# Closing a head's maxima as a task of its own, and two spacings of the maxima in place of one

## The chip, the cores and the metric

The kernel runs on one core of one Trainium2 chip. The metric is the device time of one execution in microseconds (us). The median of three runs of the kernel before is 1185.25 us, the lowest 1184.59 and the highest 1190.17.

## The reference, cut to what matters

Two layers of a streaming block. Each layer projects a normalised input into three token mixers (a retention, a latent attention with 8 heads called MLA, and a gated linear attention called GLA), gates their outputs with silu of further projections, and multiplies the result by an output matrix. The change touches only the MLA part, and there the maxima of its softmax:

```python
def block(args):
    qn, qp, i0 = args
    sc = (jnp.einsum('bqhd,bkhd->bhqk', qn, k_nope)
          + jnp.einsum('bqhd,bkd->bhqk', qp, k_pe)).astype(jnp.float32) * scale
    q_chunk = (i0 + jnp.arange(Q_BLOCK)) // CHUNK
    mask = key_chunk[None, :] <= q_chunk[:, None]
    sc = jnp.where(mask, sc, -jnp.inf)
    p = jax.nn.softmax(sc, axis=-1).astype(v.dtype)
    return jnp.einsum('bhqk,bkhe->bqhe', p, v)
```

The sequence has 1024 positions, the model 1024 columns. Everything is float32; a full product is made of three matmuls (high by high, high by low, low by high parts).

## The kernel before, in words

TensorE's work is issued in the order in which the program is written (`manual_schedule` for PE in `body`); the order of the instructions on VectorE, ScalarE, GpSimd and the DMA queue of SyncE is made by a planner, which works on a modelled time.

In `layer`, a layer runs through the retention's projections and core, the MLA's keys and queries, then a row of projections in which the rest is woven: `gk` (GLA keys), `gv` (GLA values, `proj_v`), the gates `gz0`, `gz1` of the GLA and `mz0` to `mz3` of the MLA. After these come the MLA's values `mla_v` ("mv" in the rows), its heads (`mla`, "mhead"), and the output matrix (`out_half`, "wo").

**Ticks and tasks.** After each group of three matmuls of a projection (`proj`), or of six in `proj_v`, `tick` (L527) is called. It takes 1 off the waiting count of every task in `self.tasks`, and as long as a task's count is zero or less, lets it run to its next `yield`, whose value is added to the count. A task is so woven between the matmuls of the projections. `drain` (L543) runs a task to its end on the spot, with nothing between its steps. From `gk` to the end of `mz3` there are 16 + 32 + 6 times 16 = 144 ticks.

**The maxima.** The softmax subtracts a row maximum that is found ahead of the heads by `mla_max` (L1194), started as the task `big` with a waiting count of 8 ahead of `gk`. For each of the 8 heads it makes 12 products: query block i (128 rows) against the keys up to its end, in pieces of at most 512 columns (L1245, 6 of 512 columns and 2 each of 384, 256 and 128). Each product goes into a PSUM buffer of one of two pools in turn (`maxp`, two buffers a pool, so four), and VectorE reduces it to one column (L1247). Between two products stands `yield MAXW`, 1.15 ticks. Two pairs of SBUF tiles hold the high parts of a head's queries and keys; `load(h + 1)` stands at the head's start.

**Closing a head** (`close`, L1210): VectorE reduces the head's 16 columns to 8 (L1213), 7 ticks later TensorE turns them into rows (L1217), ScalarE negates them (L1219), and a DMA writes them to `mxd` (L1220), from where `mla_stack` fetches them as a row of the head's stacked queries (L1170). Before, this runs inside `mla_max` by `yield from` ahead of the next head's third product (i == 2), so no product is made in those 7 ticks, nor in the 1.15 ticks that follow.

**Around it.** While the maxima run, the task `prep` (`gla_prep`, under `gv`) does the GLA's decay factors on VectorE, ScalarE and GpSimd ("glap"), then the task `core` (`gla_core`, under `gz0` and `gz1`, "glac") does the gated attention, then `head_out` ("hout") puts its output in place under `mz1`. In layer 0 alone, `next_chunk("k")` ahead of `mz0` adds eight reductions of `ada_w` on VectorE ("ada"). Under `mz3` the task `first` makes the first four score tiles of the MLA heads. Then `layer` fetches the stacks of heads 1 and 2 and calls `self.drain(big)`: whatever products are left are made there, one behind the other. `mla` follows: it drains `mla_v` of the first four heads, then fills seven score tiles ahead.

Of the kernel before, what the change touches and what calls it, by code (L numbers as in the profile page):

```python
# [33 lines left out]
FOLLOW = (4, 5, 6, 7)  # L34
LAG = 7
SHIFT_PE = 5
MAXW = 1.15
RW = (18, 6)

RQ, RK, RV, RZ = 0, 256, 512, 768  # L40
# [122 lines left out]
class Builder:  # L163
# [1031 lines left out]
    def mla_max(self, l):  # L1195

        nc = self.nc
        self.lab = "mmax_"
        sets = [{n: self.sl(dt=F32R, name="mx" + n) for n in "qk"} for _ in range(2)]
        for st in sets:  # L1200
            for i, n in enumerate("kq"):
                nc.sync.dma_start(st[n][96:104, :].bitcast(F32), self.mrows[i, 1:9])
            nc.sync.dma_start(st["k"][64:96, :].bitcast(F32), self.kr[l][0])

        def load(h):
            self.lab = "mmax_"
            for n in "qk":
                self.head_rows(l, h, n, 0, sets[h % 2][n])

        def close(h, mx):  # L1210
            self.lab = "mmax_"
            m8 = self.sm([128, 8])
            nc.vector.tensor_reduce(m8, mx, AX.X, ALU.max)  # L1213
            yield 7
            self.lab = "mmax_"
            ps = self.ps()
            nc.tensor.matmul(ps[0:8, 0:128], m8, self.cst("ident"), start=True, stop=True)  # L1217
            mr = self.smp.tile([8, 128], F32R, tag="mr", name=self.nm("mr"), bufs=2)
            nc.scalar.activation(mr, ps[0:8, 0:128], AF.Copy, scale=-1.0)  # L1219
            nc.sync.dma_start(self.mxd[l][h].rearrange("o (a b) -> (o a) b", a=8), mr.bitcast(F32))  # L1220

        load(0)
        done = None
        for h in range(MH):
            yield MAXW
            st = sets[h % 2]
            if h + 1 < MH:
                load(h + 1)
            self.lab = "mmax_"
            mx = self.smp.tile([128, 8, 2], F32, tag="mx", name=self.nm("mx"), bufs=2)  # L1230
            nc.gpsimd.memset(mx, NEG)
            for i in range(8):
                n = 128 * (i + 1)
                for j in range((n + 511) // 512):
                    if i or j:
                        yield MAXW
                    if i == 2 and done:
                        yield from close(*done)
                        done = None
                        yield MAXW  # L1240
                    self.lab = "mmax_"
                    w = min(512, n - 512 * j)
                    ps = self.ps(self.maxp[self.nmx % len(self.maxp)])
                    self.nmx += 1
                    nc.tensor.matmul(ps[:, :w], st["q"][0:104, 128 * i:128 * i + 128],  # L1245
                                     st["k"][0:104, 512 * j:512 * j + w], start=True, stop=True)
                    nc.vector.tensor_reduce(mx[:, i, j:j + 1], ps[:, :w], AX.X, ALU.max)  # L1247
            done = (h, mx)
        self.task(close(*done), 8)

    def mla_scores(self, h, hf, j):
# [217 lines left out]
    def layer(self, l, src):  # L1469
        nc = self.nc  # L1470
        self.chunks.extend([(l, 4), (l, 5)] + ([(l + 1, i) for i in (0, 2, 1, 3)] if l + 1 < DEPTH else []))
        mixed = [None] * 8
        self.maxp = ("mm", "s")
        if l > 0:
            self.banks = ("pj", "s", "acc")
            self.rx = self.ret_first(l, self.after_out)
# [45 lines left out]
        for i in range(2):  # L1522
            mixed[6 + i] = self.proj_silu(l, f"gz{i}")
            self.next_chunk("jk"[i])
        mz = [self.proj_silu(l, "mz0")]
        self.drain(core)
        self.maxp = ("mm", "s")
# [61 lines left out]
```

## Time and profile before

| what | value |
|---|---|
| median of three runs | 1185.25 us |
| the profiled execution, its time | 1184.63 us |
| its span, first to last instruction | 1182.8 us |
| TensorE busy | 1128.0 us, 95% of the span |
| VectorE busy | 796.7 us, 67% |
| ScalarE busy | 596.6 us, 50% |
| GpSimd busy | 529.5 us, 45% |
| mean granted TensorE clock | 0.977 of full speed |

Rows of the trace are in us from the span's start. A row of the timeline has start, duration, engine, line, operation, output and inputs, and in brackets the idle time of the engine ahead of it and what ended it. PE is TensorE, DVE VectorE, ACT ScalarE, POOL GpSimd, SPq the DMA queue of SyncE. A matmul's duration overlaps its neighbours; its price in a stream is the distance from start to start.

### The profile page before, as it was taken

How to read it: one execution, taken by the hardware profiler on the slowest of the kernel's cores; microseconds unless marked ns; L12 is line 12 of the kernel's file. 1: busy time of each engine (PE TensorE's matmuls, PEld its weight loads, DVE VectorE, ACT ScalarE, POOL GpSimd, SP SyncE). 2: the span in 40 equal slices, each digit the busy share in tenths (PEclk: the TensorE clock that was granted, in tenths of full speed). 3: DMA queues.
4: the chain of work that ended last, by engine and by line, in shares of the span. 5: the costliest groups of instructions: out<-in, count | busy, mean ns of one | idle time of the engine just before them, and what ended most of it. 6: DMA issues, size and time to landing. Idle time of an engine off the chain costs nothing.

```text
span 1182.8 us, 16979 instructions
## 1 busy us (share of the span) xinstructions
PE 1128.0 (95%) x5968; PEld 942.6 (80%) x5968; DVE 796.7 (67%) x1366; ACT 596.6 (50%) x1164; POOL 529.5 (45%) x459
## 2 busy tenths in 40 slices
PE   6999999998999899999999999999899999999996
PEld 4878977787878688887887898778788868888896
DVE  7866595686675656768875476666675666686754
ACT  6434334433545578853543434434256447886431
POOL 0064153643443346673555333444553334668620
PEclk8899999998999899999999999999999989999998
DMA  9816563651136434248453356355111653424722
GB/s 370 296 48 194 170 225 133 187 170 41 42 120 201 119 90 108 64 152 302 169 183 99 99 172 238 99 184 157 41 41 41 195 134 90 108 63 163 249 88 72
DMA packets 65585, 169.01 MB, mean 143 GB/s; under 512 B 10262, under 2 KB 13334, under 8 KB 65500
## 3 DMA queue, kind: packets, MB, share of 16 engines
q1 hardware_dynamic: 65500, 167.93, 44.7%
q8 instruction: 47, 0.77, 0.3%
q14 instruction: 38, 0.31, 0.1%
HBM read 125.36 MB, written 38.41 MB: 138 GB/s over the span
## 4 chain that ended last, share of the span: by engine, by line
PE 75%; DVE 12%; ACT 4%; DMA 4%; issue 3%; POOL 1%; SPq 0%; DVEq 0%; ACTq 0%; POOLq 0%
PE mhead_psacc L1296 3%; PE mhead_psacc L1294 3%; PE mhead_psacc L1295 3%; PE wo_pspj L558 2%; PE wo_pspj L556 2%; PE wo_pspj L557 2%; PE pmz_pspj L556 2%; PE wo_pss L557 2%; PE wo_pss L556 2%; PE wo_pss L558 2%; PE pmz_pspj L557 2%; PE pmz_pspj L558 2%; DVE mmax_mx L1247 2%; PE mhead_pss L1263 2%; PE mhead_pss L1262 2%
## 5 line engine op out<-in xcount | busy, mean ns | idle before, releaser
L457 POOL TENSOR_TENSOR wwo_wl<-wwo_wst,wwo_wh 128x1024 fp32r<-128x1024 f32 x27 | 69.0, 2559 | 40.6 <-ACT wwo_wh L456 40.5
L1271 POOL TENSOR_TENSOR mhead_wh<-mhead_p,mhead_wh 128x384 fp32r<-128x384 f32 (+1 forms) x48 | 58.1, 1211 | 56.7 <-DVE mhead_wh L1270 56.7
L1247 DVE TENSOR_REDUCE mmax_mx<-mmax_psmm 128x1 f32<-128x512 f32 (+1 forms) x96 | 57.3, 596 | 26.4 <-PE mmax_psmm L1245 25.6
L576 DVE SCALAR_TENSOR_TENSOR ada_aw<-ada_aw,silrow 128x512 f32<-128x512 f32 x64 | 62.0, 986 | 18.5 <-DMA ada_aw<-awc 18.2
L1276 DVE TENSOR_TENSOR mhead_ph<-mhead_pss,mhead_ph 128x512 fp32r<-128x512 f32 x48 | 33.1, 689 | 38.6 <-ACT mhead_pss L1275 38.6
L556 PE MATMUL pmz_pspj<-mkh_h,wmz_wh 128*128 128x512 f32 x128 | 52.5, 410 | 0.0
L1271 POOL TENSOR_TENSOR mhead_wl<-mhead_p,mhead_wl 128x128 fp32r<-128x128 f32 (+1 forms) x48 | 35.8, 746 | 34.1 <-DVE mhead_wl L1270 34.1
L557 PE MATMUL pmz_pspj<-mkh_h,wmz_wh 128*128 128x512 f32 x128 | 50.3, 393 | 0.0
L558 PE MATMUL pmz_pspj<-mkh_h,wmz_wl 128*128 128x512 f32 x128 | 50.1, 392 | 0.0
L558 PE MATMUL wo_pspj<-gran_mx,wwo_wl 128*128 128x512 f32 (+1 forms) x120 | 44.8, 374 | 1.7 <-POOL wwo_wl L457 1.7
L556 PE MATMUL wo_pspj<-gran_mx,wwo_wh 128*128 128x512 f32 (+1 forms) x120 | 45.3, 377 | 0.2 <-ACT wwo_wh L456 0.2
L1245 PE MATMUL mmax_psmm<-mmax_mxk,mmax_mxq 104*128 104x512 f32 (+1 forms) x96 | 38.9, 408 | 6.6 <-DVE mmax_mx L1247 5.9
L557 PE MATMUL wo_pspj<-gran_mx,wwo_wh 128*128 128x512 f32 (+1 forms) x120 | 44.8, 373 | 0.0
L556 PE MATMUL wo_pss<-gran_mx,wwo_wh 128*128 128x512 f32 (+1 forms) x120 | 44.6, 371 | 0.0
L558 PE MATMUL wo_pss<-gran_mx,wwo_wl 128*128 128x512 f32 (+1 forms) x120 | 44.1, 368 | 0.0
L557 PE MATMUL wo_pss<-gran_mx,wwo_wh 128*128 128x512 f32 (+1 forms) x120 | 44.1, 368 | 0.0
L600 ACT ACTIVATE ssq_sq<-ssq_x 128x512 f32<-128x512 f32 (+1 forms) x31 | 16.5, 534 | 51.7 <-DVE ssq_x L1373 51.7
L457 POOL TENSOR_TENSOR wrk_wl<-wrk_wst,wrk_wh 128x1024 fp32r<-128x1024 f32 x3 | 8.1, 2688 | 76.0 <-ACT wrk_wh L456 76.0
L1247 DVE TENSOR_REDUCE mmax_mx<-mmax_pss 128x1 f32<-128x256 f32 (+2 forms) x72 | 36.5, 507 | 7.5 <-PE mmax_pss L1245 6.8
L605 DVE TENSOR_TENSOR ssq_sq<-ssq_sq,ssq_sq 128x512 f32<-128x512 f32 (+1 forms) x30 | 30.5, 1017 | 14.0 <-ACT ssq_sq L600 14.0
L556 PE MATMUL pv_pspj<-wgv_wh,mkh_h 128*128 128x256 f32 x128 | 38.5, 301 | 0.0
L1274 ACT ACTIVATE mhead_ph<-mhead_pss 128x512 fp32r<-128x512 f32 x48 | 28.6, 596 | 17.6 <-PE mhead_pss L1264 17.0
(565 smaller groups left out, 4140.6 us busy)
## 6 DMA issues: line engine op xcount, KB each, us to landing
ada_aw<-awc SPq DMA_DIRECT2D x64, 256.0 KB
wwo_wst<-wo SPq DMA_DIRECT2D x32, 512.0 KB
aw<-awc SPq DMA_DIRECT2D x11, 512.0 KB
x<-xT SPq DMA_DIRECT2D x8, 512.0 KB
kn<-mk_ph SPq DMA_DIRECT2D x16, 256.0 KB
kn<-mk_pl SPq DMA_DIRECT2D x16, 256.0 KB
qn<-mq_ph SPq DMA_DIRECT2D x16, 256.0 KB
qn<-mq_pl SPq DMA_DIRECT2D x16, 256.0 KB
```

The lines of the kernel that those rows point to most:

```text
L457: (eng or nc.gpsimd).tensor_tensor(lo, src, hi.bitcast(F32), ALU.subtract)
L556: mm(ps, lh, rh, start=start, stop=False)
L557: mm(ps, lh, rl, start=False, stop=False)
L558: self.last = mm(ps, ll, rh, start=False, stop=stop)
L576: step = nc.vector.scalar_tensor_tensor(v, v, 1.0, self.silrow[:, cs], ALU.mult, ALU.mult, accum_out=t[:, 2 * j + i:2 * j + i + 1])
L1245: nc.tensor.matmul(ps[:, :w], st["q"][0:104, 128 * i:128 * i + 128], st["k"][0:104, 512 * j:512 * j + w], start=True, stop=True)
L1247: nc.vector.tensor_reduce(mx[:, i, j:j + 1], ps[:, :w], AX.X, ALU.max)
L1271: nc.gpsimd.tensor_tensor(pl, p, ph.bitcast(F32), ALU.subtract)
L1276: nc.vector.tensor_tensor(pl, s, ph.bitcast(F32), ALU.subtract)
L1294: mm(acc[:, o], vh, ph, start=(j == 0), stop=False, skip_group_check=True)
L1295: mm(acc[0:64, o], vl, ph, start=False, stop=False, skip_group_check=True)
L1296: mm(acc[:, o], vh, pl, start=False, stop=last, skip_group_check=True)
```

## The change

Three things are changed, for both layers:

- `close` becomes a task of its own, added ahead of the next head's second product (i == 1), so that products go on beside it. Its TensorE step stands 6 ticks behind its reduction (7 before). The extra `yield` behind it goes.
- The spacing is `self.maxw`: 1.45 ticks from the start of the layer, and 0.95 from the end of `gz1` on (1.15 throughout before).
- Nothing else: the products, reductions, pools of PSUM, and the place of `drain(big)` are the same.

```diff
-MAXW = 1.15
+MAXW = (1.45, 0.95)
@@ close, in mla_max
             nc.vector.tensor_reduce(m8, mx, AX.X, ALU.max)
-            yield 7
+            yield 6
@@ the loop over heads, blocks and pieces, in mla_max
-            yield MAXW
+            yield self.maxw
...
                     if i or j:
-                        yield MAXW
-                    if i == 2 and done:
-                        yield from close(*done)
+                        yield self.maxw
+                    if i == 1 and done:
+                        self.task(close(*done))
                         done = None
-                        yield MAXW
@@ layer
-        self.maxp = ("mm", "s")
+        self.maxp, self.maxw = ("mm", "s"), MAXW[0]
...
         for i in range(2):
             mixed[6 + i] = self.proj_silu(l, f"gz{i}")
             self.next_chunk("jk"[i])
+        self.maxw = MAXW[1]
         mz = [self.proj_silu(l, "mz0")]
```

Stepping the tick rule by hand gives the number of products (L1245) that are made in each stretch of a layer:

| stretch | ticks | products before | products after |
|---|---|---|---|
| gk | 16 | 6 | 5 |
| gv | 32 | 20 | 22 |
| gz0 | 16 | 8 | 11 |
| gz1 | 16 | 7 | 11 |
| mz0 | 16 | 9 | 17 |
| mz1 | 16 | 12 | 17 |
| mz2 | 16 | 6 | 13 |
| mz3 | 16 | 7 | 0 |
| drain behind mz3 | 0 | 21 | 0 |

## Rows read from the trace of the kernel before

**Rows 1.** The page, part 1: engine, busy us, share of the span, instructions.
```profile
PE 1128.0 (95%) x5968; PEld 942.6 (80%) x5968; DVE 796.7 (67%) x1366; ACT 596.6 (50%) x1164; POOL 529.5 (45%) x459
```

**Rows 2.** Timeline of TensorE, layer 0, from the last of mz3 to the heads.
```profile
391.38 0.34 PE L1245 MATMUL mmax_psmm<-mmax_mxk,mmax_mxq 104*128 104x384 f32 x1
...
398.16 0.60 PE L1217 MATMUL mmax_psmm<-cst,mmax_sm 128*8 128x128 f32 x2 [2.02 <-DVE mmax_sm L1213]
...
403.03 0.41 PE L556 MATMUL mv_pspj<-wukvv_wh,pmz_lat 128*128 128x256 f32 x1
...
407.44 0.40 PE L1262 MATMUL mhead_pss<-pmz_stkqh,pmz_stkkh 105*128 105x512 f32 x1
```

**Rows 3.** Timeline of VectorE in the same stretch: reductions one behind the other.
```profile
392.24 0.68 DVE L1247 TENSOR_REDUCE mmax_mx<-mmax_pss 128x1 f32<-128x512 f32 x1
392.83 0.68 DVE L1247 TENSOR_REDUCE mmax_mx<-mmax_psmm 128x1 f32<-128x512 f32 x1
```

**Rows 4.** Timeline of TensorE, layer 1, the same place.
```profile
955.49 0.34 PE L1245 MATMUL mmax_psmm<-mmax_mxk,mmax_mxq 104*128 104x384 f32 x1
...
967.14 0.42 PE L556 MATMUL mv_pspj<-wukvv_wh,pmz_lat 128*128 128x256 f32 x1
...
972.00 0.28 PE L558 MATMUL mv_pspj<-wukvv_wh,pmz_lat 128*128 128x256 f32 x1
972.12 0.40 PE L1262 MATMUL mhead_pss<-pmz_stkqh,pmz_stkkh 105*128 105x512 f32 x1
```

**Rows 5.** Stages of 2 us: PE, PEld, DVE, ACT, POOL busy, PEclk, DMA share, GB/s.
```profile
276.00:278.00 2.00, 2.00 (x10) 2.00 (x11) 1.84 (x5) 0.00 (x0) 0.07 (x1) 0.50 0.31 109
...
312.00:314.00 2.00, 2.00 (x8) 1.52 (x7) 0.08 (x1) 0.97 (x2) 0.52 (x1) 0.54 0.60 129
...
394.00:396.00 2.00, 1.63 (x6) 0.74 (x4) 2.00 (x5) 0.16 (x1) 0.00 (x0) 1.00 0.73 166
...
398.00:400.00 2.00, 1.84 (x5) 1.25 (x6) 0.69 (x4) 0.27 (x1) 0.35 (x2) 0.50 0.91 223
```

**Rows 6.** Timeline of TensorE in mz2 of layer 1: only the maxima shown.
```profile
937.38 0.39 PE L1245 MATMUL mmax_psmm<-mmax_mxk,mmax_mxq 104*128 104x512 f32 x1
938.31 0.22 PE L1245 MATMUL mmax_pss<-mmax_mxk,mmax_mxq 104*128 104x128 f32 x1
939.11 0.40 PE L1245 MATMUL mmax_psmm<-mmax_mxk,mmax_mxq 104*128 104x512 f32 x1
```

**Rows 7.** Stages of layer 0 (columns as in Rows 5): gv with prep, then mz0 and mz1.
```profile
251.00:276.00 25.00, 21.60 (x161) 19.65 (x159) 23.27 (x41) 9.31 (x21) 12.04 (x14) 0.97 0.26 75
335.00:365.00 30.00, 28.34 (x135) 22.60 (x134) 26.24 (x53) 13.78 (x27) 11.48 (x9) 1.00 0.59 189
```

**Rows 8.** The same stages, the maxima's tile alone: DVE busy, POOL busy, PEclk, DMA.
```profile
251.00:276.00 25.00, 5.86 (x13) 0.12 (x1) 0.97 0.26 75
335.00:365.00 30.00, 10.92 (x23) 0.23 (x2) 1.00 0.59 189
```

**Rows 9.** Timeline of TensorE, layer 0: its waits under gv, gz0 and mz0.
```profile
272.33 0.50 PE L1245 MATMUL mmax_pss<-mmax_mxk,mmax_mxq 104*128 104x512 f32 x1 [1.07 <-DVE mmax_mx L1247]
275.87 0.48 PE L1245 MATMUL mmax_psmm<-mmax_mxk,mmax_mxq 104*128 104x128 f32 x1 [2.33 <-DVE mmax_mx L1247]
...
311.03 1.10 PE L1009 MATMUL glac_psacc<-pv_v,pgz_gat 128*128 128x64 f32 x8 [1.68 <-DVE mmax_mx L1247]
...
341.95 0.33 PE L1245 MATMUL mmax_psmm<-mmax_mxk,mmax_mxq 104*128 104x128 f32 x1 [0.37 <-DVE mmax_mx L1247]
```

**Rows 10.** Timeline of ScalarE behind mz3 in layer 0: the silu of mz3's second half.
```profile
392.20 0.63 ACT L430 ACTIVATE pmz_zt<-pmz_mz 128x512 f32<-128x512 f32 x1
...
393.53 0.63 ACT L432 ACTIVATE pmz_zt<-pmz_zt 128x512 f32<-128x512 f32 x1
```

**Rows 11.** Queue of SyncE behind mz3 in layer 0: last row of head 1's stack.
```profile
391.30 0.44 SPq L1170 DMA_DIRECT2D pmz_stkqh<-mxd  x1
```

**Rows 12.** The chain that ended last, around 227 us: a fetch of a head's queries.
```profile
226.96 3.60 DMA mmax_mxq<-qr
```

## What the change was predicted to do

> **What bounds the kernel now.** I read the page's engine rows first: TensorE is busy for 95% of the span, VectorE for 67% [rows 1]. So an edit pays only where TensorE stands still, runs at its lower clock, or both, and the question is where that is. Then the timeline of TensorE around the maxima, which shows it twice, once a layer. Behind `mz3` the products that the ticks did not reach are made by `drain(big)` with nothing between them, from 391.38 to 403.03 us in layer 0 and from 955.49 to 967.14 in layer 1 [rows 2, 4]: 11.65 us each. VectorE sets the pace there: a reduction of 512 columns starts 0.59 us after the one ahead [rows 3], and the close of head 6 waits 2.02 us for its reduction with no other work to do [rows 2]. The stages of 2 us show what comes next: the clock is 1.00 at 394 and 0.50 at 398, that is 2.4 and then 1.2 GHz [rows 5], and the matmuls of `mv` that follow still feel it. Third, the stages of `gv` and of `mz0` and `mz1`: there VectorE is busy for 23.27 of 25 us and 26.24 of 30 [rows 7], and TensorE waits for reductions, 1.07 and 2.33 us under `gv`, 1.68 in the gated attention, 0.37 under `mz0` [rows 9]. So the change takes products out of a stretch bound by VectorE, and puts them in stretches where VectorE is nearly full as well.
>
> **What goes: the drained stretch.** By the table of products none is left for the drain; head 7's last product is made 19 ticks before `mz3` ends. TensorE's order is the written one, so this part does not hang on the planner. The 22 products from 391.38 on (the first of them falls on the last tick) are 12 of 512 columns, 4 of 384, 3 of 256, 3 of 128. In a stream, 937.38 to 938.31 holds a product of 512 columns and three matmuls of 512: 0.93 us, so 0.23 for each; 938.31 to 939.11 holds one of 128 and three of 512, so 0.80 less 0.69 = 0.11 [rows 6]. With 0.19 and 0.15 for the sizes between, 22 products are 2.76 + 0.76 + 0.45 + 0.33 = 4.3 us, and the close is 0.3 (0.60 at half the clock [rows 2]). That work moves, it does not go; 11.65 less 4.6 is 7.05 us a layer. `mv`'s 24 matmuls take 4.41 us (403.03 to 407.44) and 4.98 (967.14 to 972.12) where 24 at 0.12 (972.00 to 972.12) would be 2.88 [rows 2, 4]: 1.5 and 2.1 more. Together 14.1 + 3.6 = **17.7 us** to gain.
>
> **What it costs, first: the seam behind mz3.** What is late next once the drain is gone? `mv` starts at once, and ScalarE, which has to take its results out of PSUM, is then in the silu of the last half of `mz3`, 392.20 to 394.16 [rows 10]; the drain covered that. `mv` has two PSUM buffers, so its third group waits for the first to be taken out. If the planner puts the silu first, as it is written, TensorE waits up to its 1.96 us; if not, nothing. I take 1.25 a layer, nearer to the written order: **2.5 us** (0 to 3.9). The last row of head 1's stack is issued at 391.30 [rows 11]; a fetch of queries took 3.60 us to land [rows 12], which would be 394.9, and the first need is the end of `mv`, 391.4 + 2.9 + 1.25 = 395.5. That is just in time, so nothing, with up to 1 us in the range.
>
> **Second: mz0 and mz1 in layer 0.** 34 products against 21 in these 32 ticks. 23 reductions took 10.92 us there, 0.475 each [rows 8], so 13 more are 6.2 us: VectorE's 26.24 become 32.4, while TensorE's 30 become 32.6 by the products' own 2.6. Full to the rim, with four PSUM buffers as the only slack; `ada`, the eight reductions that only layer 0 has here, can lie anywhere. Waits of 0 to 4 us, **2** taken; none in layer 1.
>
> **Third: gv.** Of VectorE's 23.27 us, 5.86 are 13 maxima [rows 7, 8], so 17.4 are other work, above all `prep`, written in two lumps at ticks 21 and 25. Before, the close left ticks 26 to 33 without a product, just beside the first lump; now six are made there, and 19 instead of 16 between ticks 21 and 48. Three more at 0.45 are 1.35 us in a stretch that VectorE already sets, and the early ones stand behind the lump. I take **1.5 a layer, 3.0**. It can be below nothing: at 1.45 ticks the products come thinner beside the second lump, where TensorE waited 3.4 us [rows 9] and the clock was then 0.50 [rows 5]. Half of that wait and clock back would be 3 us a layer; the other end is the slower rival's.
>
> **Fourth: the gated attention.** 22 products against 15 share its PSUM pools "mm" and "acc"; one wait of 1.68 us stands there [rows 9]. Half a us a layer, **1.0** (from one such wait less to one more in each layer).
>
> **Edits at nothing.** The close's own steps are the same; its TensorE step comes 6 ticks behind its reduction, some 5 us in which projections and products run, where the drain gave it none. Behind it on TensorE stand the projection's matmuls, so a late reduction would hold these. Its write to `mxd` waits in SyncE's queue ahead of other fetches as before. A head now takes 12 times 0.95 = 11.4 ticks, some 10 us, and its fetch is issued when the head before it starts: 3.60 us to land [rows 12] leaves 6 for the queue.
>
> **The clock.** The low clock stood behind TensorE's idle time of 3.4 us in `gv` and behind the 1.68 us wait (0.54 at 312), but not behind the thin waits in the first half of the drain, where it was 1.00 at 394 [rows 5, 9]. The Trainium skill, "TensorE: Matmul & The Clock Gate", section "A second HAM failure mode: psum-queue depth-cycling", speaks against the change here: an engine that idles a little and often between groups, while it goes round its PSUM buffers, can swing between the two clocks though no single gap is long. By rows 5 thin waits cost only themselves and the sum stands; by the rule the dense maxima would cost what the second rival says.
>
> **The sum.** Gain 17.7, given back 2.5 + 2 + 3 + 1 = 8.5: net 9.2. The profiled execution took 1184.63 us (span 1182.8, 1.8 around it, unchanged), so 1175.4; it lies 0.6 under the median of 1185.25, which makes **1176.0 us**.
>
> **The rivals.**
> - *Full relief, 1167 us (1162 to 1171).* The planner spreads the reductions, the seam and the gates cost under 2 us together, and the waits under `gv` shrink with the wider spacing, by up to 3 us a layer. For it: the four buffers and the even spacing. Against it: VectorE is over 87% busy at each place.
> - *The gates take it back, 1183 us (1180 to 1186).* VectorE's queue in `mz0` and `mz1` puts `ada` and the GLA's closing steps ahead of reductions, TensorE waits 4 us or more there and falls to the low clock. At an average clock of 0.75 over 30 us that is 30 / 0.75 less 30 = 10 us in place of the 2 of the sum, 8 more than forecast. The page's rule named above leads here too, without a long wait; the rows speak against it. For the rival: 32.4 in 32.6 us. Against it: before, at 88% busy, the only wait for a reduction in `mz0` was 0.37 us [rows 9].
> - *Slower: prep's lumps hold TensorE, 1192 us (1190 to 1197).* If the planner runs the lumps ahead of the reductions, TensorE can go four products on, some 4.9 us at 1.45 ticks, then stands until 17.4 us of VectorE work are done: 12.5 us in place of 3.4, 9.1 more a layer, 18.2 in all. With the other costs (5.5) that is 23.7 against 17.7; and some of the clock on top. It decides from a growth of the wait of (17.7 - 5.5) / 2 = 6.1 us a layer. For it: now no pause lies beside the first lump. Against it: in the trace the planner put single reductions between the lumps' steps, 13 of them in those 25 us [rows 8].
> - *The drain stays.* Only if products were left over; the counts leave 19 ticks. No chance worth a number.
>
> **How the numbers follow.** Forecast 0.50 (1171 to 1180), full relief 0.20, gates 0.20, slower 0.10. Half a per cent, 5.9 us, is about what a measurement of this kernel can tell from no change: faster is under 1179.3, slower over 1191.2. Nearly all of the forecast and the relief are faster: 0.70; the gates, the forecast's upper end and the slower rival's lower end are the same: 0.21; slower 0.09. The range from 1166 to 1186 takes in the forecast, the gates and most of the relief, and leaves out the slower rival and the relief's lower end, some 0.17.
>
> **What would show it.** Between the last matmul of `mz3` and the first of `mv` no product stands, and the clock there is 1.00. `mv` takes 3 to 5 us in each layer; over that, the seam was taken too low. TensorE's waits on L1247 under `gv`: about 5 us a layer if the third term holds, 12 for the slower rival, under 2 for the relief. Under `mz0` and `mz1` VectorE over 95% busy in layer 0, well below in layer 1, and TensorE's waits there 2 us. The forecast is wrong above all if the planner's new order of VectorE moves waits to where the trace of before has none.

## The result, and the profile after

The kernel after takes 1170.08 us (median; 1166.24 to 1171.95) against 1186.32 us for the kernel before in the same comparison (1184.59 to 1190.17): a ratio of 0.9858, 95% interval 0.983 to 0.9885, so 1.4% faster. The profiled execution took 1170.77 us, with a span of 1169.0.

The engine rows of the page, which answer to [rows 1]:

```profile
PE 1117.3 (96%) x5968; PEld 937.6 (80%) x5968; DVE 792.6 (68%) x1366; ACT 596.0 (51%) x1164; POOL 527.0 (45%) x459
```

The instructions are as many as before; TensorE is busy for 10.7 us less. Where that comes from is seen stage by stage. In the table a stage lasts from the first matmul of its tiles to the first of the next stage's, on the timeline of TensorE; "seam" is from the first matmul of `mv` to the first product of probabilities and values (L1293), so it holds `mv`'s 24 matmuls and the 12 matmuls of the four score tiles behind them.

| stage | layer 0 before | after | layer 1 before | after |
|---|---|---|---|---|
| gk | 13.96 | 13.73 | 13.89 | 13.73 |
| gv | 36.47 | 32.63 | 34.98 | 31.48 |
| gz0, gz1 (gated attention) | 53.34 | 51.37 | 51.16 | 51.35 |
| mz0 to mz3, and the drain | 69.38 | 63.58 | 67.22 | 59.52 |
| seam | 6.31 | 10.09 | 6.86 | 11.24 |
| the heads behind it | 105.34 | 105.08 | 105.30 | 104.84 |

So the drain is gone, `gv` is shorter where I expected it longer, and 3.8 and 4.4 us were handed back at the seam. Timeline of TensorE in the kernel after, from `gv` to the heads of layer 0, and in the last row the seam of layer 1; it answers to [rows 2, 4, 9]:

```profile
250.59 1.09 PE L908 MATMUL glap_psacc<-turn_pt,glap_wg 48*128 48x512 f32 x2 [1.12 <-DMA glap_wg<-wg]
...
266.25 0.50 PE L1244 MATMUL mmax_psmm<-mmax_mxk,mmax_mxq 104*128 104x512 f32 x1 [0.42 <-DVE mmax_mx L1246]
267.45 0.39 PE L1217 MATMUL mmax_psmm<-cst,mmax_sm 128*8 128x128 f32 x2 [0.69 <-DVE mmax_mx L1246]
...
337.11 0.49 PE L1244 MATMUL mmax_psmm<-mmax_mxk,mmax_mxq 104*128 104x512 f32 x1 [0.71 <-DVE mmax_mx L1246]
339.08 0.39 PE L1217 MATMUL mmax_psmm<-cst,mmax_sm 128*8 128x128 f32 x2 [1.47 <-DVE mmax_sm L1213]
...
392.60 0.40 PE L558 MATMUL pmz_pspj<-mkh_h,wmz_wl 128*128 128x512 f32 x1
392.83 0.29 PE L556 MATMUL mv_pspj<-wukvv_wh,pmz_lat 128*128 128x256 f32 x1
...
398.25 0.58 PE L556 MATMUL mv_pspj<-wukvv_wh,pmz_lat 128*128 128x256 f32 x1 [3.60 <-DVE pmz_vl L1191]
...
400.97 0.46 PE L1261 MATMUL mhead_pss<-pmz_stkqh,pmz_stkkh 105*128 105x512 f32 x1
...
402.92 0.44 PE L1293 MATMUL mhead_psacc<-mhead_ph,pmz_vh 128*128 128x512 f32 x1
...
955.44 0.58 PE L556 MATMUL mv_pspj<-wukvv_wh,pmz_lat 128*128 128x256 f32 x1 [3.60 <-DVE pmz_vl L1191]
```

To be seen there: the last matmul of `mz3` and the first of `mv` stand next to each other, with no product between; the third group of `mv` then waits 3.60 us in each layer; and of the waits for maxima under `gv` only 0.42 and 0.69 us are left (0.42 and 0.70 in layer 1).

Timeline of ScalarE at the same seam:

```profile
393.03 0.59 ACT L717 COPY pmz_mz<-pmz_pspj 128x512 f32<-128x512 f32 x1 [0.41 <-PE pmz_pspj L558]
393.65 0.63 ACT L430 ACTIVATE pmz_zt<-pmz_mz 128x512 f32<-128x512 f32 x1
394.31 0.63 ACT L431 ACTIVATE pmz_zt<-pmz_zt 128x512 f32<-128x512 f32 x1
394.98 0.63 ACT L432 ACTIVATE pmz_zt<-pmz_zt 128x512 f32<-128x512 f32 x1
396.36 0.63 ACT L434 ACTIVATE pmz_zu<-pmz_zu 128x512 f32<-128x512 f32 x1 [0.76 <-DVE pmz_zu L433]
396.90 1.05 ACT L1190 CAST pmz_vh<-mv_pspj 128x512 fp32r<-128x512 f32 x2
```

The wait of TensorE is put down to VectorE (L1191), but L1191 subtracts what the cast L1190 made, and the cast stands in ScalarE's queue behind the copy of `mz3`'s last half, three steps of its silu, a step on VectorE for which ScalarE waits 0.76 us, and a fourth step.

Stages of 25 and 2 us of the kernel after (PE, PEld, DVE, ACT, POOL busy, PEclk, DMA share, GB/s), which answer to [rows 5, 7]:

```profile
252.60:277.60 25.00, 23.89 (x178) 21.89 (x178) 24.28 (x45) 9.03 (x20) 11.40 (x14) 1.00 0.24 68
277.00:279.00 2.00, 2.00 (x14) 1.82 (x13) 1.97 (x6) 1.10 (x2) 0.07 (x1) 1.00 0.50 141
312.00:314.00 2.00, 2.00 (x15) 1.78 (x14) 1.44 (x5) 0.00 (x0) 1.01 (x2) 1.00 0.00 0
340.00:342.00 2.00, 2.00 (x6) 1.63 (x6) 2.00 (x6) 0.04 (x1) 0.21 (x2) 0.50 0.47 136
...
398.00:400.00 2.00, 1.75 (x8) 1.76 (x9) 0.79 (x2) 0.07 (x1) 2.00 (x5) 0.50 0.96 221
...
957.00:959.00 2.00, 2.00 (x9) 1.83 (x9) 0.69 (x1) 1.17 (x2) 2.00 (x5) 0.50 1.04 236
```

The granted clock is 1.00 where it was 0.50 and 0.54 [rows 5], and 0.50 behind the two new places that wait: `mz0` of layer 0, and the seam of both layers. The second line of the same kind, for the maxima alone, answers to [rows 8]:

```profile
252.60:277.60 25.00, 8.47 (x17) 0.11 (x1) 1.00 0.24 68
```

With 17 maxima in these 25 us in place of 13, VectorE is busy for 24.28 us in place of 23.27: 2.61 us of maxima more, and only 1.01 us of busy time more.

### The profile page after: what moved, and what is told of

Read it like the earlier page. It is cut to its first block, busy times and chain, and to the rows that moved or that the text cites. A ratio compares the mean times of both kernels' runs of the same rounds, so it can differ in the third digit from the quotient of the medians.

```text
span 1169.0 us, 16968 instructions
## 1 busy us (share of the span) xinstructions
PE 1117.3 (96%) x5968; PEld 937.6 (80%) x5968; DVE 792.6 (68%) x1366; ACT 596.0 (51%) x1164; POOL 527.0 (45%) x459
## 4 chain that ended last, share of the span: by engine, by line
PE 74%; DVE 12%; DMA 5%; ACT 4%; issue 4%; POOL 1%; SPq 0%; DVEq 0%; ACTq 0%; POOLq 0%
PE mhead_psacc L1295 3%; PE mhead_psacc L1293 3%; PE mhead_psacc L1294 3%; PE pmz_pspj L556 3%; PE pmz_pspj L557 2%; PE pmz_pspj L558 2%; DMA ada_aw<-awc 2%; PE wo_pspj L558 2%; PE wo_pspj L556 2%; PE wo_pspj L557 2%; PE wo_pss L558 2%; PE wo_pss L556 2%; PE wo_pss L557 2%; PE mhead_pss L1262 2%; PE mhead_pss L1261 2%
## 5 line engine op out<-in xcount | busy, mean ns | idle before, releaser
L1262 PE MATMUL mhead_pss<-pmz_stkql,pmz_stkkh 96*128 96x512 f32 x96 | 36.6, 381 | 0.0
L1261 PE MATMUL mhead_pss<-pmz_stkqh,pmz_stkkh 105*128 105x512 f32 x96 | 36.6, 381 | 0.0
```

The source lines that it names most:

```text
L1261: mm(s, st["kh"][0:105, ks], st["qh"][0:105, qs], start=True, stop=False)
L1262: mm(s, st["kh"][0:96, ks], st["ql"][0:96, qs], start=False, stop=False)
```

## The experiments

### One part at a time: the close, and the spacing

The close as a task of its own, with the old spacing throughout:

```diff
-MAXW = (1.45, 0.95)
+MAXW = (1.15, 1.15)
```

> The close as a task of its own, but the spacing 1.15 throughout as before. By the tick rule nothing is left to drain, and 24 products fall into ticks 21 to 48 (16 before, 19 in the changed kernel). Theory (the number of reductions against VectorE's room decides under gv): 8 more reductions of 0.45 us than before are 3.6 us in a stretch that VectorE already fills, so TensorE waits 5 to 7 us there and falls to 1.2 GHz; gv lasts 38 to 41 us in each layer (36.47 and 34.98 before, 32.63 and 31.48 in the changed kernel), and the whole 1178 to 1184 us. Rival (the even stream makes the planner mix the reductions into the GLA's preparation, whatever their number): gv lasts 32 to 35 us, and the whole 1168 to 1173 us.

Measured: 1171.26 us (1168.99 to 1172.27), ratio 0.9867 (0.9847 to 0.9887): within the intervals, as much as the whole change. `gv` took 34.27 and 33.49 us with 28 products in it, where the kernel before made 20 in 36.47 and 34.98. So the number of reductions under `gv` does not decide: the theory fell, and both times lie where the rival put them. Timeline of TensorE in this run, its longest waits for maxima in layer 0:

```profile
274.98 0.39 PE L1217 MATMUL mmax_psmm<-cst,mmax_sm 128*8 128x128 f32 x2 [1.26 <-DVE mmax_mx L1246]
...
341.17 0.39 PE L1217 MATMUL mmax_psmm<-cst,mmax_sm 128*8 128x128 f32 x2 [2.40 <-DVE mmax_sm L1213]
```

Then the spacing alone, with the close still inside `mla_max` (the kernel before, with these lines):

```diff
-MAXW = 1.15
+MAXW = (1.45, 0.95)
...
+        self.maxw = MAXW[1]
         mz = [self.proj_silu(l, "mz0")]
```

> The two spacings of the changed kernel, but the close inside the maxima as before, with its pause. By the tick rule 13 products fall into ticks 21 to 48 and 22 are left to drain (21 before). Theory: the gain is made of two parts that can be had one by one, the end of the drained stretch (by the task) and the relief under gv (by the spacing): here the drain stays with its 11.65 us, gv falls to 31 to 33 us in each layer, and the whole is 1177 to 1181 us. Rival (the task gives both): gv stays at 35 to 37 us and the whole at 1185 to 1188 us.

Measured: 1176.56 us (1174.71 to 1178.73), ratio 0.9909 (0.9885 to 0.9933). `gv` took 33.50 and 32.17 us with 16 products; the drain stays (`mz0` to the drain's end 71.03 and 68.52 us) and the seam has none of the cost (6.86 and 6.70). Both parts of the theory are there, and its time is 0.4 us under the range, but the parts do not add up: 15 us by the task alone, 10 by the spacing alone, 16 by both. Two of the waits, on TensorE's timeline of layer 0:

```profile
277.54 0.68 PE L1245 MATMUL mmax_psmm<-mmax_mxk,mmax_mxq 104*128 104x512 f32 x1 [2.19 <-DVE mmax_mx L1247]
...
395.80 0.60 PE L1217 MATMUL mmax_psmm<-cst,mmax_sm 128*8 128x128 f32 x2 [1.22 <-DVE mmax_sm L1213]
```

To compare the two, `gv` of layer 1 is brought to the change's 22 products at 0.2 us each (between the 0.11 and 0.23 of [rows 6]): before 35.4, the task alone 32.3, the spacing alone 33.4, both 31.5. So each part by itself takes away half or more of the excess under `gv` (3.1 and 2.0 us of 3.9), and the two overlap. What costs is the pause together with close products: without the pause (28 products), or with wider ones (16 products), half or more of the cost is gone. These are stages of one trace each.

Why the busy time in [rows 7] was no measure of room shows beside GpSimd. One product of `prep`, L930, is recorded on VectorE with 1167 ns before, 906 after, 838 with the spacing alone and 680 with the task alone (means of two in layer 0). Timelines of GpSimd and VectorE in layer 0, first of the kernel before, then with the task alone:

```profile
258.64 1.74 POOL L936 TENSOR_TENSOR glap_gqn<-pgq_gq,glap_gt 128x512 f32<-128x512 f32 x1
259.26 1.40 DVE L930 TENSOR_TENSOR glap_gkm<-pgk_gk,glap_gel 128x256 f32<-128x256 f32 x1
```

```profile
258.47 1.74 POOL L936 TENSOR_TENSOR glap_gqn<-pgq_gq,glap_gt 128x512 f32<-128x512 f32 x1
259.09 0.69 DVE L1246 TENSOR_REDUCE mmax_mx<-mmax_pss 128x1 f32<-128x512 f32 x1
259.81 0.68 DVE L930 TENSOR_TENSOR glap_gkm<-pgk_gk,glap_gel 128x256 f32<-128x256 f32 x1
```

Before, L930 ends at 260.66, 0.28 us behind the end of L936 on GpSimd. With the task alone a reduction stands ahead of it, it starts 0.55 us later, and it ends at 260.49: again 0.28 us behind L936. In all 13 traces, both layers and both halves, 52 records of 0.68 to 1.40 us, it ends 0.28 or 0.29 us behind L936, whenever it starts, though the two share no tile. By these ends, part of what [rows 7] show as busy is VectorE standing until GpSimd is through, and a reduction put into that time cost `prep` nothing here: L930 ended no later. Why the one holds the other, no run here shows. `prep`'s 28 steps on VectorE are recorded with 19.1 us in all before, 18.0 after and 16.8 with the task alone. From the first of them to the last are 23.74 us before (10 maxima inside), 23.48 with the spacing alone (8), 24.37 after (14) and 24.83 with the task alone (19): nearly twice the maxima for 1.1 us.

### The spacing under the output gates

```diff
-MAXW = (1.45, 0.95)
+MAXW = (1.45, 1.3)
```

> The changed kernel with 1.3 in place of 0.95 as the spacing under the output gates: 12, 13, 12 and 10 products under mz0 to mz3 in place of 17, 17, 13 and 0, none left to drain. Theory (dense maxima beside the eight reductions of ada_w fill VectorE under mz0 of layer 0 and cost 2.2 us of waits and the clock behind them): these waits fall below 0.8 us in layer 0, nothing changes under mz0 in layer 1, the seam stays at 3.6 us or grows by the reductions that now stand beside it, and the whole is 1166 to 1170 us. Rival (the closer spacing is needed, products under mz3 share PSUM and VectorE with the first score tiles): the seam grows by 1 to 3 us a layer and the whole is 1171 to 1175 us.

Measured: 1170.76 us (1169.84 to 1172.95), ratio 0.9868 (0.9848 to 0.9888), and `mz0` to `mz3` 63.11 and 59.24 us against 63.58 and 59.52. The wait of 3.60 us at the seam is there as well, and under `mz0` of layer 0 one wait of 2.23 us on TensorE's timeline:

```profile
340.21 0.39 PE L1217 MATMUL mmax_psmm<-cst,mmax_sm 128*8 128x128 f32 x2 [2.23 <-DVE mmax_sm L1213]
```

So the theory was wrong, as the waits stay, and the rival too, as the seam does not grow. The closer spacing that the change chose for the output gates is worth nothing that can be measured; the run with a spacing of 1.55, below, is faster.

### The seam: the PSUM buffers, or ScalarE's queue

First, more PSUM: `mv`'s first four heads use a second pool as well, for two of their four groups (t = 2 and 6, not for three of four as the expectation has it), so that no group of `mv` has to wait for a cast.

```diff
-            ps = self.ps("pj", (128, 2, 256))
+            ps = self.ps("acc" if g == 0 and t % 4 else "pj", (128, 2, 256))
```

> The changed kernel, with the first four value tiles behind mz3 in two PSUM pools (pj, then acc three times out of four) in place of pj alone, so that TensorE need not wait for the third. Theory (at the seam TensorE waits 3.60 us for a PSUM buffer that ScalarE, busy with the silu, has not emptied): the wait shrinks below 1.5 us a layer, its low clock goes, from the first of mv to the heads' first value product 5 to 7 us (10.09 and 11.24 in the changed kernel, 6.31 and 6.86 before), and the whole is 1161 to 1165 us. Rival (ScalarE's queue is the bound, the wait moves to the first score tiles or values behind it): mv shorter, the heads' start no earlier by more than 1 us, the whole 1168 to 1171 us.

Measured: 1172.67 us (1171.65 to 1173.5), ratio 0.9881 (0.9863 to 0.9899); from `mv`'s first matmul to L1293 9.23 and 9.09 us, and the heads 2.6 and 2.0 us longer. Timelines of TensorE, ScalarE and VectorE in layer 0:

```profile
401.75 0.77 PE L1293 MATMUL mhead_psacc<-mhead_ph,pmz_vh 128*128 128x512 f32 x1 [3.39 <-DVE pmz_vl L1191]
```

```profile
399.38 0.59 ACT L1190 CAST pmz_vh<-mv_pspj 128x512 fp32r<-128x512 f32 x1
```

```profile
400.93 0.67 DVE L1191 TENSOR_TENSOR pmz_vl<-mv_psacc,pmz_vh 128x512 fp32r<-128x512 f32 x1
```

`mv` itself waits no more: its 24 matmuls start 0.12 us apart, from 392.52 to 395.27. The wait has moved to the first product with the values, and the clock is 0.50 from 402 to 408. Two things that came with the edit make it. The planner put the four casts behind four exponentials of the heads and the silu's last step, from 399.38 in place of 396.90; and this product needs a buffer of the pool that the edit gave to `mv`, and starts 0.15 us behind the L1191 that empties one (401.60). So the theory fell: more buffers alone do not bring the time. That buffers play no part is not shown by this run.

Then the queue itself. The silu of `mz3`'s second half is held back, and issued behind the four casts of `mv`'s first four heads:

```diff
... in proj_silu, with late=True for mz3 alone
-            self.silu(v, v, self.pt(name="zt"), self.pt(name="zu"), self.nc.gpsimd)
+            if late and hf:
+                self.late = v
+            else:
+                self.silu(v, v, self.pt(name="zt"), self.pt(name="zu"), self.nc.gpsimd)
... in mla_v
-            nc.scalar.copy(hv, ps.rearrange("p t (a e) -> p t a e", a=4))
+            self.cast = nc.scalar.copy(hv, ps.rearrange("p t (a e) -> p t a e", a=4))
... in mla, behind the drain of mla_v
+        with self.tc.issue_after(self.cast.ins):
+            self.silu(self.late, self.late, self.pt(name="zt"), self.pt(name="zu"), nc.gpsimd)
```

> The kernel after, with the silu of the second half of mz3 issued behind the four casts of mv's first four heads on ScalarE. Theory (ScalarE's queue order makes the seam: in the kernel after, the first cast of mv runs only behind a copy, the silu's steps, their wait for VectorE and a last exponential, at 396.90 us): the wait of 3.6 us of TensorE at the seam falls under 0.5 us in each layer, the clock stays 1.00 there, and mv takes 5 to 7 us in place of 10.1 and 11.2; the heads start their exponentials behind the silu and lose 1 to 2 us of it. Whole 1161 to 1165 us. Rival (the heads' first tiles need ScalarE just as early, so the wait moves behind them, as it did with the other PSUM buffers): the heads grow by 3 to 4 us a layer, whole 1168 to 1172.

Measured: 1165.16 us (1160.63 to 1169.1), ratio 0.9825 (0.9794 to 0.9856). The seam fell to 5.92 us in both layers, and the heads grew by 3.5 and 3.4. TensorE's timeline in layer 0:

```profile
396.68 0.39 PE L556 MATMUL mv_pspj<-wukvv_wh,pmz_lat 128*128 128x256 f32 x1 [0.46 <-DVE pmz_vl L1194]
...
402.90 0.61 PE L1264 MATMUL mhead_pss<-pmz_stkqh,pmz_stkkh 105*128 105x512 f32 x1 [1.68 <-DVE mhead_ph L1278]
```

Both were right in part: the queue makes the seam, and the silu, put right ahead of the heads' exponentials, holds the heads. So the silu goes further back, behind the exponentials of the first two units of the heads, in place of behind the casts:

```diff
... in mla_scores
-            nc.scalar.activation(p, s, AF.Exp, scale=ATT_SCALE)
+            self.cast = nc.scalar.activation(p, s, AF.Exp, scale=ATT_SCALE)
... in mla, at the end of each unit (h, hf)
+            if (h, hf) == (1, 0):
+                with self.tc.issue_after(self.cast.ins):
+                    self.silu(self.late, self.late, self.pt(name="zt"), self.pt(name="zu"), nc.gpsimd)
```

> The kernel after, with the same silu moved still further back: behind the exponentials of the first two units of heads (one further unit than the start of the heads). Theory (ScalarE's order at the seam): mv 5 to 7 us, the heads unchanged within 1 us, since ScalarE has slack there; whole 1160 to 1164 us, some 8 below the kernel after. Rival (ScalarE is not the bound but VectorE's share of the casts, or the low clock comes anyway): mv over 9 us, whole 1168 to 1172.

Measured: 1162.29 us (1161.01 to 1163.43), ratio 0.9802 (0.9787 to 0.9816). The seam takes 5.91 and 5.92 us, the heads 104.80 and 104.82, as in the kernel after (105.08, 104.84). Timelines of TensorE and of ScalarE in layer 0:

```profile
397.50 0.39 PE L556 MATMUL mv_pspj<-wukvv_wh,pmz_lat 128*128 128x256 f32 x1 [0.46 <-DVE pmz_vl L1194]
...
399.26 0.40 PE L1264 MATMUL mhead_pss<-pmz_stkqh,pmz_stkkh 105*128 105x512 f32 x1
```

```profile
396.14 0.59 ACT L1193 CAST pmz_vh<-mv_pspj 128x512 fp32r<-128x512 f32 x1
...
411.13 0.61 ACT L430 ACTIVATE mhead_zt<-pmz_mz 128x512 f32<-128x512 f32 x1
```

The first cast runs 0.91 us behind the first matmul of `mv` (395.23) instead of 4.07, the 3.60 us wait is 0.46, and the silu's first step, at 411.13, holds nobody. ScalarE's order at the seam is thereby shown to cost 4.2 and 5.3 us (10.09 and 11.24 less 5.9), 9.5 in all; the low clock behind the wait is part of it. Of the eight seams that were traced with the silu in its place, six took 10.1 to 10.4 us and two, both in layer 1, 11.24 and 11.55; in the kernel after the clock there was still 0.53 from 959 to 961. The whole fell by 7.8 us only, as `mz0` to `mz3` of layer 0 took 65.30 us in this trace in place of 63.58.

The other way to cover the queue is to leave a little of the drain standing:

```diff
-MAXW = (1.45, 0.95)
+MAXW = (1.45, 1.55)
```

> The kernel after, with a spacing of 1.55 ticks in place of 0.95 under mz0 to mz3, so that 6 products are left for the stretch between mz3 and mv. Theory (the drain that is left gives ScalarE the time it lacks at the seam): 6 products at VectorE's pace of 0.59 us take 3.5 us and take the place of most of the wait of 3.6 us; the clock stays 1.00, mv falls from 10.1 and 11.2 to 6 to 8 us, mz0 to mz3 with the drain about 1 us longer less 2 us for the products that leave it; whole 1164 to 1168 us. Rival (the drain is as dear as what it hides: close waits there for VectorE, 2.02 us in the trace of before): mz0 to mz3 with the drain 3 us longer in each layer, whole 1168 to 1173.

Measured: 1162.38 us (1160.64 to 1163.48), ratio 0.9801 (0.9787 to 0.9816), below both ranges. TensorE's timeline and a stage of the same run in layer 0:

```profile
395.93 0.39 PE L556 MATMUL mv_pspj<-wukvv_wh,pmz_lat 128*128 128x256 f32 x1 [1.60 <-DVE pmz_vl L1191]
```

```profile
394.00:396.00 2.00, 0.40 (x4) 0.20 (x2) 2.00 (x5) 1.45 (x3) 0.17 (x2) 1.00 0.94 234
```

Six products and a close fill the time from 390.46 to 392.73, 2.27 us where their own price is some 1.6 by [rows 6]; the wait behind them is 1.60 us, and the clock stays 1.00. The casts now start at 393.65, ahead of the silu's last step (395.23), and it is VectorE, at the reductions until 394.60, that comes to L1191 only at 395.19. The seam took 6.61 and 6.60 us, and `mz0` to `mz3` with these products 61.70 and 59.79. A drain of six costs 0.7 us over its own work, one of 22 cost 7 us a layer. My reading, argued and not tried by itself: the four PSUM buffers take up the first products, and only then does VectorE's pace show.

And did the silu cost the kernel before something too? The same deferral, put into the kernel before:

> The kernel before with the silu of mz3's second half behind the first two units of heads, and nothing else changed. Theory (the drained stretch of 11.65 us hid ScalarE's queue there, and what mv lost before was the low clock alone): mv unchanged at 6 to 7 us, whole 1184 to 1187 us, no difference. Rival (ScalarE's queue cost mv something before as well, so that part of what the silu's place gives is no cost of the change): mv under 5.9 us and the whole 2 to 5 us lower.

Measured: 1185.09 us (1180.78 to 1190.1), ratio 0.9988 (0.9972 to 1.0004): no difference. The seam takes 6.53 and 6.86 us (before 6.31 and 6.86). Why it makes no difference shows on ScalarE's timeline of the kernel before, in layer 0, with the silu in its place:

```profile
396.33 0.63 ACT L434 ACTIVATE pmz_zu<-pmz_zu 128x512 f32<-128x512 f32 x1 [2.17 <-DVE pmz_zu L433]
...
404.52 1.31 ACT L1190 CAST pmz_vh<-mv_pspj 128x512 fp32r<-128x512 f32 x2 [5.46 <-PE mv_pspj L558]
```

There the silu's last step ends at 396.96, under the drain, and ScalarE stands idle for 5.46 us ahead of the first cast (5.49 with the silu deferred). So the drain did hide the silu, and the cost at the seam is one of the change.

### mz0 in layer 0

Layer 0's eight reductions of `ada_w` go from ahead of `mz0` to behind `mz1`; nothing else is moved.

```diff
-CHUNKS = "ccgkno"
+CHUNKS = "ccgmno"
```

> The kernel after, with layer 0's eight reductions of ada_w moved from ahead of mz0 to behind mz1. Theory (ada's reductions stand ahead of the maxima on VectorE and make the two waits of 0.71 and 1.47 us of TensorE under mz0 of layer 0, and the clock of 0.50 and 0.73 behind them): these waits fall under 0.8 us together, mz0 to mz3 of layer 0 take 60 to 61 us in place of 63.6, layer 1 is unchanged, whole 1166 to 1169 us. Rival (the same lump now makes the same wait under mz2, where products are as close): mz0 to mz3 unchanged at 63 to 64 us, whole 1169 to 1172.

Measured: 1168.1 us (1166.18 to 1173.93), ratio 0.9862 (0.9829 to 0.9895). The whole alone would not tell it from the kernel after; the stage does: `mz0` to `mz3` of layer 0 took 60.42 us in place of 63.58. TensorE's timeline, the only wait left in these gates of layer 0, and a stage of the same run:

```profile
371.78 0.39 PE L1244 MATMUL mmax_pss<-mmax_mxk,mmax_mxq 104*128 104x256 f32 x1 [0.53 <-DVE mmax_mx L1246]
```

```profile
338.00:342.00 4.00, 4.00 (x20) 2.90 (x19) 2.77 (x6) 2.60 (x5) 0.89 (x1) 1.00 0.01 1
```

The waits of 0.71 and 1.47 us are gone, the clock is 1.00, and the lump makes 0.53 under `mz2`. So `ada` was the cause, and it cost 3.2 us: two more traces with `ada` in its place, those of the second PSUM pool and of the silu behind the casts, have 63.58 too, and the next run with `ada` behind `mz1` has 60.42 again. It can cost more: in the run with the silu later the close waited 2.12 us there, and these gates took 65.30.

### Together

The silu behind the first units of the heads and `ada` behind `mz1`:

> The kernel after with both: the silu of mz3's second half behind the first two units of heads, and layer 0's reductions of ada_w behind mz1. Theory (the seam and ada are two separate costs): mv 5.9 us in each layer, mz0 to mz3 of layer 0 60 to 61 us in place of 65.3 in the run with the silu alone, so 3 to 5 us under that run's 1162.3: whole 1157 to 1160 us. Rival (what ada costs is made up elsewhere, by other waits of layer 0): whole 1161 to 1163.

Measured: 1157.33 us (1156.09 to 1160.03), ratio to the kernel before 0.9758 (0.9741 to 0.9776): faster than both kernels, 2.4% under before. The seam takes 5.91 us in each layer, `mz0` to `mz3` of layer 0 60.42. The page's engine rows of this run:

```profile
PE 1111.2 (96%) x5968; PEld 931.4 (81%) x5968; DVE 799.0 (69%) x1366; ACT 595.2 (52%) x1164; POOL 527.3 (46%) x459
```

And the two cheapest edits together, the spacing of 1.55 and `ada` behind `mz1`:

> The kernel after with a spacing of 1.55 ticks under mz0 to mz3 (six products left for the drain) and layer 0's reductions of ada_w behind mz1. Theory: mz0 to mz3 with the drain 59 to 60 us in layer 0 in place of 61.7, mv 6.6 in each layer; whole 1159 to 1162 us. Rival (at this wider spacing the products are too thin for ada to hold any, and only its own luck of the planner decides): unchanged, 1162 to 1164.

Measured: 1161.41 us (1160.15 to 1163.01), ratio 0.979 (0.9775 to 0.9805). `mz0` to `mz3` with the six products took 60.88 us in layer 0 (61.70 without `ada`'s move), so little of `ada`'s price is left at the wider spacing, as the rival said, and the whole is within the theory's range and 1.0 us under the run with the spacing alone, inside its interval; `gv` of layer 0 was 34.61 in this run, for a reason told at the end.

## Why the prediction was right, and where its steps were wrong

The time fell within the range and on the side forecast, 0.5% under the predicted time; it is 0.9 us below the forecast's own stretch (1171 to 1180), where the full relief begins. But the sum came near because two of its terms were wrong by 9 and 11 us in opposite directions, which is luck. The prediction's terms, put on the stages of the table above (a moved product counted at 0.2 us), against what the traces show, both layers together:

| stage | forecast us | measured us |
|---|---|---|
| mz0 to mz3 and the drain: 2 x 7.05 and the 8 products a layer that leave it, less 2 | -15.3 | -13.5 |
| gv: 3.0 and 2 products more a layer | +3.8 | -7.3 |
| gated attention: 1.0 and 7 products more a layer | +3.8 | -1.8 |
| gk: one product less a layer | -0.4 | -0.4 |
| seam: 2.5 less 3.6 | -1.1 | +8.2 |
| all else | 0 | +1.0 |
| sum | -9.2 | -13.8 |

**The drained stretch** was read rightly: no product stands between `mz3` and `mv`. Of the 7.05 us a layer 6.1 are gone in layer 1 (67.22 less 59.52, less 1.6 for the 8 products), and 7.4 in layer 0 once `ada` is out of the way (60.42).

**The seam** was the right place and the right mechanism, mis-sized by a factor of nearly four: 1.25 us a layer was taken, 4.2 and 5.3 were measured. The step that failed is the bound "up to its 1.96 us". It counted the silu's steps up to the third (L432) on ScalarE in [rows 10]; the trace of before had a fourth, L434 at 396.33 behind a wait of 2.17 us for VectorE (shown above). What stands between `mz3`'s last matmul and the first cast is the whole queue: the copy, the silu's steps, its turn on VectorE with the wait for it, and one exponential more, from 393.03 to 396.90, which is 3.87 us in the kernel after. And the low clock that follows a wait of 3.60 us, which I had named elsewhere, was not added here. The text had said what over 5 us of `mv` would mean, and `mv` took 8.14 and 8.15 (392.83 to 400.97 in layer 0). A second step failed in the same row: the 3.6 us that `mv` was to gain from 24 matmuls at 0.12. With the silu out of the way and a clock of 1.00 they take 4.03 us (395.23 to 399.26), not 2.88, with a wait of 0.46 for the casts (0.12 throughout was reached only with the second PSUM pool); and in layer 0 of the kernel before, part of the excess was such a wait on TensorE's timeline, not the clock:

```profile
405.88 0.39 PE L556 MATMUL mv_pspj<-wukvv_wh,pmz_lat 128*128 128x256 f32 x1 [0.68 <-DVE pmz_vl L1191]
```

So there were 1.3 us to gain (the seam at 5.9 against 6.31 and 6.86). The 9.3 us between forecast and measurement in the table are the 7.0 of the queue and the 2.3 of this.

**gv** failed in its step "a stretch that VectorE already sets". The rows were right, VectorE was busy for 23.27 of 25 us, but part of that was standing behind GpSimd, and it did not mean that nothing more fits: 17 maxima went through where 13 had, in nearly the same time. The end below nothing of that term (3 us a layer back) was the right one, and the measured gain passes it. The full relief's reason, the four buffers and the even spacing, was the better reading of this stretch: the waits for maxima fell to 1.1 us a layer, under the 2 that it named, and the run with the task alone shows the even spacing at work with 28 products under `gv`; the part of the buffers was not tried. The slower rival rested on the same wrong step.

**The gated attention**: of 1.9 us of waits a layer 0.8 are left, and the one of 1.68 us is gone, so layer 1 took only 0.19 more for 7 more products. The term had the wrong sign, by the same mistake in small. But the 1.97 us less of layer 0 are in part the clock of one execution (0.54 at 312 before, 1.00 after): layer 1 of the kernel before had the same wait and kept 1.00, as shown at the end.

**mz0 and mz1 of layer 0**: 2 us taken, 3.2 measured, inside the bounds of 0 to 4, none in layer 1, and by the cause that was named, `ada` on VectorE. The gates that take it back did not come: 17 products each in `mz0` and `mz1` made no wait beyond these, and VectorE's 26.24 us of 30 did not become 32.4: it was busy for 26.12 of the same 30 us (330.6 to 360.6), with 14.86 of maxima in place of 10.92. In layer 1 the same dense maxima ran without any wait, and the clock was 1.00 from 891.8 to 921.8. So the rule of the Trainium skill weighed there ("TensorE: Matmul & The Clock Gate", "A second HAM failure mode: psum-queue depth-cycling") did not show in this kernel.

**The edits at nothing** were not all nothing: the close's TensorE step, 6 ticks behind its reduction, waited 1.47 us for its reduction at 339.08, and 0.69 for a PSUM buffer at 267.45, with the projection's matmuls queued behind it, as the text had said a late reduction would do. The first of these two was `ada`'s doing as well.

The rest, +1.0, lies in stretches that the change does not touch: the first 230 us differed by 1.64 us between the two profiled executions, and by up to 3.7 us among all 13.

## What to carry to other kernels

When a stretch in which one engine drains work is taken away, list all that the other engines still have queued at its end, in queue order and with their waits for each other, and price the seam by the whole queue; here a silu on ScalarE turned 11.65 us of cover into a wait of 3.60 us, and moving it behind the first heads was worth 8 us of the whole. A high busy share of an engine is no proof that it is full: see whether its records end with another engine's, ask whether the work that it would get is spread evenly against what waits for it, and try it. A few products left for a gap that another engine makes are cheaper than none and than many: six filled it, 22 cost 7 us a layer.

## What the runs showed that I had not expected

Two things. The same instruction on VectorE is recorded with 0.68 to 1.40 us, by when GpSimd ends, as shown above.

And behind the same wait TensorE's clock falls in one execution and not in another. The row at 250.59 of the kernel after, with its wait of 1.12 us for a transfer, and the stages behind it:

```profile
252.00:254.00 2.00, 2.00 (x18) 1.96 (x17) 1.52 (x3) 1.21 (x3) 0.00 (x0) 1.00 0.89 300
254.00:256.00 2.00, 2.00 (x13) 1.44 (x11) 1.60 (x3) 0.84 (x2) 0.00 (x0) 1.00 0.14 57
```

The run with the silu behind the casts, whose `gv` is the same program, with the same wait of 1.07 us:

```profile
250.75 1.09 PE L911 MATMUL glap_psacc<-turn_pt,glap_wg 48*128 48x512 f32 x2 [1.07 <-DMA glap_wg<-wg]
```

```profile
252.00:254.00 2.00, 2.00 (x13) 1.96 (x13) 1.29 (x2) 1.21 (x3) 0.00 (x0) 0.74 0.79 270
254.00:256.00 2.00, 2.00 (x9) 1.94 (x9) 0.56 (x1) 0.78 (x2) 0.00 (x0) 0.50 0.30 120
```

So `gv` of layer 0 took 32.6 to 32.8 us in some runs and 34.0 to 34.6 in others with the same spacing and order there, and 31.47 to 31.49 in layer 1 of all of these, which has no wait for the transfer.

The gated attention of the kernel before has the same: its wait of 1.68 us in layer 0, with 0.54 behind it [rows 5, 9], stands in layer 1 of the same trace too, and there the clock is 1.00:

```profile
878.98 1.10 PE L1009 MATMUL glac_psacc<-pv_v,pgz_gat 128*128 128x64 f32 x8 [1.69 <-DVE mmax_mx L1247]
```

```profile
880.00:882.00 2.00, 2.00 (x15) 1.80 (x14) 0.85 (x3) 1.35 (x4) 0.46 (x1) 1.00 0.53 119
```

With the silu deferred in the kernel before, that stretch of layer 1 fell to 0.50 (882 to 884), and took 53.38 us in place of 51.16. A stage's time in one trace can carry some 2 us of this.
